# A hybrid attention layer: another buffer for v's turned tiles, weight splits kept, output weights issued earlier, and the next rows' squares moved to another stage

## The chip, the cores and the metric

One Trainium2 chip, one of its cores. The time is the device time of one execution in microseconds, the median of three runs. Five engines work side by side: TensorE (PE), VectorE (DVE), ScalarE (ACT), GpSimd (POOL) and SyncE (SP), which here issues every DMA. Each takes its own instructions in the order in which they were issued to it.

## The reference, cut to what matters

One decoder layer: 16 learned meta tokens stand ahead of 2048 tokens of width 1024; after a norm, one projection makes the queries, keys and values of two attention branches and four sets of gates. One branch is stick-breaking attention (8 heads), the other sliding-window attention over 128 tokens with sinks (16 query heads on 2 key and value heads).

```
def rms_norm(x, g):
    y = xf * lax.rsqrt(jnp.mean(xf * xf, axis=-1, keepdims=True) + RMS_EPS)
...
xn = rms_norm(h, norm_gain[l])
proj = xn @ w_in[l]
sb_q, sb_k, sb_v, sw_q, sw_k, sw_v, sb_z, sw_z, g_sb, g_sw = jnp.split(proj, offsets, axis=-1)
...
# stick-breaking, per head
log_beta = jax.nn.log_sigmoid(z)                       # z = q k^T * scale
log_1m = jnp.where(mask, log_beta - z, 0.0)
rev = lax.cumsum(log_1m, axis=3, reverse=True)
w = jnp.where(mask, jnp.exp(log_beta + suffix), 0.0)   # suffix: rev shifted by one
```

Each branch's output is gated, projected to width 1024 and gated again; the two are added, projected by `w_out`, added to x, and normed once more.

## The kernel before, in words

All products of float32 operands are made as three products of their split parts: each operand is split into a high part and the rest (`h` and `l`), and TensorE forms h·h, l·h and h·l (in `gemm`, L404 to L406). A split costs a copy on ACT or POOL and a difference on DVE or POOL.

The 2048 tokens are four groups of 512, worked on in two halves, first groups 2 and 3, then groups 0 and 1. Each half has three stages:

- The sliding-window stage (`window`, `attend`): projection tiles of 128 columns, each a `gemm`, are woven with the attention of the window, row by row. Here v's tiles of the stick-breaking branch are made too: TensorE turns them into PSUM (`ps_zm`, L512), ACT and DVE write the high part and the rest into the tile `vt` (allocated at L513, in a ring of one buffer), and a DMA stores `vt` to `vd` in HBM.
- The stick-breaking stage (`stick`), woven with the tiles of the gates (`gts`). For each head and group, a state, the keys, values and queries are loaded: the queries twice, as `q1` and, with halves swapped, as `q2`, each from a ring of two buffers. A state's score rows (L813) go through ACT's sigmoid (L817) and DVE's running product (L824), are turned by TensorE (L835), split (L113, L114) and multiplied with v.
- The finish: the branch projections, the product with `w_out`, and the last norm.

The order of TensorE's instructions is written out by hand. DVE's is by hand at the start only; ACT, POOL and SP are ordered by a scheduler from the order of the text, with the buffer rings as a constraint. All DMAs stand in one queue on SP.

**Weights.** `weights` (L164) serves one tile of 128 columns: the first time it loads it (512 KB, ring `raw` of two buffers), splits it, and stores high part and rest to HBM; `kept` remembers where. A later call loads the two parts. `kept.pop` forgets a tile with the second call, so that a third call loads, splits and stores again. This concerns the eight tiles of the window's queries, which are called once for each group, four times in all; the others are called twice.

**Scales of x.** The norm needs each row's sum of squares. `squares` (L346) loads 128 rows by 512 columns at a time into the ring `xs` (four buffers, which the window stage uses too), squares them on ACT with an accumulated sum, and `rsqrt` (L116) makes the scale: a logarithm (L119), an exponential (L120) and a step of refinement. For the second half's two groups, `group_scales` is called in the first half, after the tenth gate tile of the stick-breaking stage; with the ring as it is, the scheduler puts the squares into the end of the window stage before.

**Output weights.** In the finish, `w_out` is used in two column halves. `out_weights(k, ch)` loads one of eight 128-row tiles (ring `a` of six buffers), casts it on ACT (L234) and subtracts on DVE (L235). The first column half is prepared during the projection before. The second is issued after both row tiles (t = 0 and 1) of the first column half. For each row tile: TensorE's product (L280 to L282), DVE's addition of x into `res` (L284), ACT's square (L288).

Of the kernel before, what the change touches and what calls it, by code (L numbers as in the profile page):

```python
# [16 lines left out]
P = 128  # L17
# [27 lines left out]
def tile_kernel(ctx, tc, x, xt, meta, metat, gain, w_in, w_sb, w_sw, w_out, sinks, fgain,  # L45
# [67 lines left out]
        A.activation(h, acc, AF.Copy, scale=scale)  # L113
        V.scalar_tensor_tensor(l, acc, scale, f32(h), op0=ALU.mult, op1=ALU.subtract)  # L114

    def rsqrt(r, ssq, pool, mid=lambda: None):  # L116

        V.tensor_scalar(ssq, ssq, 1.0 / D, EPS, op0=ALU.mult, op1=ALU.add)
        A.activation(r, ssq, AF.Ln)  # L119
        A.activation(r, r, AF.Exp, scale=-0.5)  # L120
        mid()
        t = pool.tile([P, 4], F32, tag="nwt", name="nwt", bufs=2)[:r.shape[0], :r.shape[1]]
        V.tensor_tensor(t, r, r, op=ALU.mult)
        V.tensor_tensor(t, t, ssq, op=ALU.mult)
        V.tensor_scalar(t, t, -0.5, 1.5, op0=ALU.mult, op1=ALU.add)
        V.tensor_tensor(r, r, t, op=ALU.mult)
# [23 lines left out]
    def drain(*gens):  # L150
        for _ in chain(*gens):
            pass
# [11 lines left out]
    def weights(c0, w=w_in, raw=None):  # L164

        if c0 in ready:
            return ready.pop(c0)
        n = w.shape[2]
        wh, wl = (wp.tile([P, KT, P], F32R, tag=t, name=t, bufs=3)[:, :n, :] for t in ("wh", "wl"))
        key = w.name, c0  # L170
        if key in kept:
            for t, k in zip((wh, wl), kept.pop(key)):
                DMA(t, k)
            return wh, wl
        raw = load(c0, w) if raw is None else raw
        split(wh, wl, raw)
        kept[key] = [dram(f"{t}_{w.name}_{c0}", [P, n, P], F32R) for t in "hl"]
        for t, k in zip((wh, wl), kept[key]):
            if put_off is None:
                DMA(k, t)  # L180
            else:
                put_off.append((k, t))
        return wh, wl
# [19 lines left out]
    def finish(ringl, osw, first):  # L203
# [23 lines left out]
        for half, groups in enumerate(halves):  # L227
            part, merged, wo = {}, {}, {}

            def out_weights(k, ch):  # L230
                raw = small("a", AB)
                DMA(raw, w_out[0, k * P:(k + 1) * P, ch * GT:(ch + 1) * GT])
                h, l = wo[k, ch] = ringr(), ringr()
                A.copy(h, raw)  # L234
                V.tensor_tensor(l, raw, f32(h), op=ALU.subtract)  # L235
# [29 lines left out]
            for g in groups:  # L265
                for t0 in range(0, 4, 2):
                    res, ssq = {}, {}
                    end = (half, g, t0) == (1, groups[1], 2)
                    for ch in range(2):
                        cs = slice(ch * GT, (ch + 1) * GT)  # L270
                        for t in (t0, t0 + 1):
                            row = g * GT + t * P
                            if ch == 0:
                                res[t] = cp.tile([P, D], F32, tag="xr", name="res", bufs=3)
                                DMA(res[t], x[row:row + P, :])
                            acc = bank()
                            ts = slice(t * P, (t + 1) * P)
                            for k in range(KT):
                                (mh, ml), (wh, wl) = merged[k, g], wo[k, ch]
                                T.matmul(acc, lhsT=mh[:, ts], rhs=wh, start=k == 0, stop=False)  # L280
                                T.matmul(acc, lhsT=mh[:, ts], rhs=wl, start=False, stop=False)
                                T.matmul(acc, lhsT=ml[:, ts], rhs=wh, start=False, stop=k == KT - 1)  # L282
                            r = res[t][:, cs]
                            V.tensor_tensor(r, acc, r, op=ALU.add)  # L284
                            sq = cp.tile([P, GT], mybir.dt.bfloat16, tag="a", name="sq", bufs=AB)
                            if ch == 0:
                                ssq[t] = cp.tile([P, 2], F32, tag="ssq", name="ssq2", bufs=4)
                            A.activation(sq, r, AF.Square, accum_out=ssq[t][:, ch:ch + 1])  # L288
                            if end and t == 3:
                                V.tensor_tensor(r, r, fg[:, cs], op=ALU.mult)  # L290
                                if ch == 0:
                                    s0 = cp.tile([P, 1], F32, tag="rs", name="rs2", bufs=4)
                                    V.tensor_scalar(s0, ssq[t][:, 0:1], 1.0 / D, EPS, op0=ALU.mult, op1=ALU.add)
                        if (g, t0, ch) == (groups[0], 0, 0):
                            for k in range(KT):
                                out_weights(k, 1)
                    for t in (t0, t0 + 1):
                        row = g * GT + t * P
                        if end and t == 3:
                            s1 = ssq[t][:, 1:2]  # L300
                            rs, u = (cp.tile([P, 1], F32, tag="rs", name="rs2", bufs=4) for _ in range(2))
                            A.activation(rs, s1, AF.Ln, bias=s0, scale=1.0 / D)
                            A.activation(rs, rs, AF.Exp, scale=-0.5)
                            V.tensor_scalar(u, s1, 1.0 / D, s0, op0=ALU.mult, op1=ALU.add)
                            V.scalar_tensor_tensor(u, rs, rs, u, op0=ALU.mult, op1=ALU.mult)
                            V.tensor_scalar(u, u, -0.5, 1.5, op0=ALU.mult, op1=ALU.add)
                            a, b = (res[t][:, ch * GT:(ch + 1) * GT] for ch in range(2))
                            A.activation(a, a, AF.Copy, scale=rs)
                            V.tensor_scalar(b, b, rs, u, op0=ALU.mult, op1=ALU.mult)
                            DMA(out[row:row + P, GT:], b)  # L310
                            A.activation(a, a, AF.Copy, scale=u)
                            DMA(out[row:row + P, :GT], a)
                            continue
                        V.tensor_tensor(ssq[t][:, 0:1], ssq[t][:, 0:1], ssq[t][:, 1:2], op=ALU.add)
                        rs = cp.tile([P, 1], F32, tag="rs", name="rs2", bufs=4)
                        rsqrt(rs, ssq[t][:, 0:1], cp)
                        for ch in range(2):
                            cs = slice(ch * GT, (ch + 1) * GT)
                            V.scalar_tensor_tensor(res[t][:, cs], res[t][:, cs], rs, fg[:, cs], op0=ALU.mult, op1=ALU.mult)
                        DMA(out[row:row + P, :], res[t])  # L320
                if half == 0:
                    g2 = halves[1][g - groups[0]]
                    osw2.update({(k, g2): gated(ow, zw, k, g2, ringl, lambda: small("a", AB)) for k in range(8)})
# [32 lines left out]
    def spread(rs, rows, n):  # L356
# [2 lines left out]
        for i in range(n):  # L359
            T.transpose(acc[:, i * rows:(i + 1) * rows], rs[:rows, i:i + 1].to_broadcast([rows, P]), ident[:rows, :rows])  # L360
        return acc[:, :n * rows]

    def group_scales(g, tag="rs"):
        return scales(squares(x[g * GT:(g + 1) * GT, :], P, 4), P, 4, tag)

    def scale_rows(rs, rb=None):
        if rb is None:
# [127 lines left out]
    def sb_v(p):  # L495

        def use(g, acc, ms):
# [11 lines left out]
            def rows():  # L509
                tr = ps("zm")  # L510
                for i in range(4):
                    T.transpose(tr[:, i * P:(i + 1) * P], d[:, i * P:(i + 1) * P], ident)  # L512
                vt = tp.tile([P, 4, 2, P], F32R, tag="vt", name="vt", bufs=1)  # L513
                evac_split(vt[:, :, :, 0:64], vt[:, :, :, 64:128], tr.rearrange("p (b a d) -> p b a d", b=4, a=2))
                DMA(vd[p][g].rearrange("a p b d -> p b a d"), vt)

# [238 lines left out]
        return sw_k, sw_v, sw_q, attend, ending  # L755


    def stick(groups, bp):
        kt, vc = {}, {}
        rows_of = {}  # L760
        for g in groups:
# [34 lines left out]
        def row(h, g, n, j):  # L796

            if n == j == 0:
                load_kv(h, g)
                state[h, g] = {"q": load_q(h, g), "last": {}}  # L800
            st = state[h, g]
            last = st["last"]
            b0 = 4 * (g + n) + j
# [236 lines left out]
    for half, groups in enumerate(halves):  # L1040
# [38 lines left out]
            flush_all()  # L1079
        with tc.tile_pool(name=f"sb{half}", bufs=1, side="left") as bp:  # L1080
            vsplit[0] = False
            side = stick(groups, bp)
            drain(tiles_by_tile(gts[3:4], groups))
            rest = 25 if half == 0 else 23
            cost_sb = 8 * sum(4 * (4 - g) for g in groups) * 1.31 + 16 * 0.75
            ratio = cost_sb / ((rest - 4) * 10.4)
            left = weave(tiles_by_tile(gts[4:14], groups), side, ratio)
            if half == 0:
                rs0, rs1 = (group_scales(g) for g in halves[1])
            weave(tiles_by_tile(gts[14:rest], groups), side, ratio, left)  # L1090
            drain(side)
        if half == 0:
            ts = [mk() for mk in gts[rest:]]
            drain(by_group(ts, groups[:1]), by_group(ts[:1], groups[1:]))
# [69 lines left out]
```

## Time and the profile before

| | |
|---|---|
| median of three runs | 2207.05 us (2206.35 to 2208.54) |
| the profiled execution | 2209.05 us, its span 2207.3 us |
| mean granted clock of TensorE in it | 0.994 |
| PE busy | 2160.9 us, 98% of the span |
| DVE, ACT, POOL busy | 1365.7, 1013.8, 380.2 us |
| window stage of the first half ends | at about 400 us; its stick-breaking stage at about 773 us |

The span runs from the first to the last instruction on the core. In rows of a timeline the first number is the start, the second the time that the instruction, or the run of equal instructions counted at the end, took; brackets hold how long the engine was idle before it and what released it. In rows of groups the three durations are the shortest, the median and the longest in nanoseconds. Waits are listed as the engine, the tile and the line that waited, then the engine, the tile and the line that ended the wait, then total, count and longest.

### The profile page before, as it was taken

The page shows a single profiled execution, that of the slowest core. Times are in us where ns is not written, and L with a number is a line of the kernel's source. Part 1 is how long each engine was busy: PE and PEld are TensorE (multiplying, and loading weights), DVE is VectorE, ACT ScalarE, POOL GpSimd, SP SyncE. Part 2 cuts the span into 40 slices and gives each one's busy share as a digit, 9 for nine tenths or more (in the row PEclk, how much of TensorE's full clock was granted, in tenths as well). Part 3 has the DMA queues.
Part 4 walks back from the last instruction along what each step waited for, and adds up shares of the span by engine and source line. Part 5 has one row for each costly group of instructions (what it writes and reads, how often), then busy time and mean ns, then how long its engine had stood idle before and what let it go on. Part 6 is the DMA issues. An engine that isn't in the chain of part 4 may idle for free.

```text
span 2207.3 us, 30283 instructions
## 1 busy us (share of the span) xinstructions
PE 2160.9 (98%) x10614; PEld 1771.3 (80%) x10614; DVE 1365.7 (62%) x2130; ACT 1013.8 (46%) x2332; POOL 380.2 (17%) x493
## 2 busy tenths in 40 slices
PE   8899999999999999999999999999999999999998
PEld 6678887788888888788887888888888888787876
DVE  6678876356555443778755888778774437453543
ACT  6566767333433323677753555555553202221121
POOL 2123342322222201233310000000000232000000
PEclk9999999999999999999999999999999999999999
DMA  9655446856455365544446433333323976467422
GB/s 335 232 175 189 172 171 210 261 182 203 161 179 180 130 232 181 172 172 151 155 135 196 120 110 113 116 99 112 115 84 129 348 271 212 147 221 271 151 91 86
DMA packets 175800, 384.61 MB, mean 174 GB/s; under 512 B 23040, under 2 KB 41216, under 8 KB 175648
## 3 DMA queue, kind: packets, MB, share of 16 engines
q1 hardware_dynamic: 175648, 382.67, 52.0%
q8 instruction: 84, 1.38, 0.3%
q14 instruction: 68, 0.56, 0.1%
HBM read 233.16 MB, written 149.37 MB: 173 GB/s over the span
## 4 chain that ended last, share of the span: by engine, by line
PE 77%; issue 2%; DVE 1%; DMA 1%; ACT 1%; POOL 0%; POOLq 0%; ACTq 0%; DVEq 0%
PE ps_g L404 12%; PE ps_g L405 12%; PE ps_g L406 12%; PE ps_o L861 6%; PE ps_z L813 6%; PE ps_t L835 5%; PE ps_o L722 1%; PE ps_z L676 1%; PE ps_g L224 1%; PE ps_g L225 1%; PE ps_z L225 1%; PE ps_g L223 1%; PE ps_z L223 1%; PE ps_z L224 1%; PE ps_t L225 1%
## 5 line engine op out<-in xcount | busy, mean ns | idle before, releaser
L404 PE MATMUL ps_g<-xh,wh 128*128 128x512 f32 x1544 | 639.2, 414 | 9.7 <-ACT xh L911 7.5
L405 PE MATMUL ps_g<-xl,wh 128*128 128x512 f32 x1544 | 609.2, 395 | 0.4 <-DVE xl L912 0.4
L406 PE MATMUL ps_g<-xh,wl 128*128 128x512 f32 x1544 | 608.9, 394 | 0.0
L824 DVE TENSOR_TENSOR_SCAN row<-row 128x512 f32<-128x512 f32 (+2 forms) x320 | 372.5, 1166 | 176.4 <-POOL row L822 105.1
L406 PEld LDWEIGHTS ps_g<-xh,wl 128*128 128x128 f32 x1544 | 291.7, 189 | 65.5
L404 PEld LDWEIGHTS ps_g<-xh,wh 128*128 128x128 f32 x1544 | 293.4, 190 | 57.3 <-ACT xh L911 7.5
L405 PEld LDWEIGHTS ps_g<-xl,wh 128*128 128x128 f32 x1544 | 293.2, 190 | 43.9 <-DVE xl L912 0.9
L817 ACT ACTIVATE row<-ps_z 128x512 f32<-128x512 f32 (+1 forms) x320 | 172.0, 538 | 276.2 <-PE ps_z L813 228.7
L114 DVE SCALAR_TENSOR_TENSOR wtl<-ps_t,wth 128x512 fp32r<-128x512 f32 (+1 forms) x320 | 189.8, 593 | 42.9 <-ACT wth L113 41.4
L113 ACT ACTIVATE wth<-ps_t 128x512 fp32r<-128x512 f32 (+1 forms) x320 | 170.4, 532 | 97.4 <-PE ps_t L835 95.8
L813 PE MATMUL ps_z<-kt,q 128*128 128x512 f32 (+3 forms) x640 | 185.0, 369 | 0.3 <-ACT row L817 0.3
L835 PE MATMUL ps_t<-ident,row 128*128 128x128 f32 x1088 | 171.6, 273 | 1.2 <-DVE row L824 1.2
L835 PEld LDWEIGHTS ps_t<-ident,row 128*128 128x128 f32 x1088 | 135.9, 140 | 37.3 <-DVE row L824 1.7
L109 POOL TENSOR_SCALAR wh<-raw 128x1024 fp32r<-128x1024 f32 (+1 forms) x71 | 75.8, 1067 | 437.6 <-PE ps_g L405 303.7
L822 POOL TENSOR_SCALAR_AFFINE_SELECT row<-row 128x128 f32<-128x128 f32 x128 | 44.1, 346 | 619.0 <-ACT row L817 584.0
L813 PEld LDWEIGHTS ps_z<-kt,q 128*128 128x128 f32 x640 | 118.7, 188 | 26.4 <-ACT row L817 0.8
L861 PE MATMUL ps_o<-wth,vc 128*128 128x512 f32 (+1 forms) x320 | 125.7, 393 | 1.3 <-DVE tmp L866 1.1
L552 ACT ACTIVATE tmp<-ps_g 128x512 f32<-128x512 f32 x112 | 67.1, 599 | 121.0 <-PE ps_g L406 113.9
L684 ACT ACTIVATE sc<-sc,nm 128x129 f32<-128x129 f32 x256 | 100.0, 392 | 37.0 <-DVE nm L682 36.4
L861 PE MATMUL ps_o<-wtl,vc 128*128 128x512 f32 (+1 forms) x320 | 116.8, 365 | 0.0
L110 POOL TENSOR_TENSOR wl<-raw,wh 128x1024 fp32r<-128x1024 f32 (+1 forms) x43 | 96.4, 2242 | 3.1
L262 ACT CAST ringl<-gt 128x512 fp32r<-128x512 f32 x32 | 19.9, 621 | 132.0 <-DVE gt L260 128.0
(293 smaller groups left out, 3457.8 us busy)
## 6 DMA issues: line engine op xcount, KB each, us to landing
raw<-in_w_in SPq DMA_DIRECT2D x58, 512.0 KB, 4.5
h_in_w_in<-wh SPq DMA_DIRECT2D x58, 512.0 KB, 3.2
l_in_w_in<-wl SPq DMA_DIRECT2D x58, 512.0 KB, 3.4
wh<-h_in_w_in SPq DMA_DIRECT2D x58, 512.0 KB, 3.7
wl<-l_in_w_in SPq DMA_DIRECT2D x58, 512.0 KB, 4.8
q<-qd SPq DMA_DIRECT2D x128, 128.0 KB, 3.4
vc<-vd SPq DMA_DIRECT2D x48, 256.0 KB, 2.7
kd<-tmp SPq DMA_DIRECT2D x32, 256.0 KB, 4.1
```

The costliest lines, as they stand in the source:

```text
L110: (V if vsplit[0] else G).tensor_tensor(l, src, f32(h), op=ALU.subtract)
L113: A.activation(h, acc, AF.Copy, scale=scale)
L114: V.scalar_tensor_tensor(l, acc, scale, f32(h), op0=ALU.mult, op1=ALU.subtract)
L404: T.matmul(acc, lhsT=wh[:, k, :], rhs=xh[g][:, k, :], start=k == 0, stop=False)
L405: T.matmul(acc, lhsT=wh[:, k, :], rhs=xl[g][:, k, :], start=False, stop=False)
L406: T.matmul(acc, lhsT=wl[:, k, :], rhs=xh[g][:, k, :], start=False, stop=k == KT - 1)
L684: A.activation(sc[:, hh, :], sc[:, hh, :], AF.Exp, bias=nm[:, hh:hh + 1], accum_out=den[:, hh:hh + 1])
L813: T.matmul(z[:, :w], lhsT=lq, rhs=kt[h][:, k0:k0 + w], start=t == 0, stop=t == 1)
L817: A.activation(r[:, :w], z[:, :w], AF.Sigmoid, scale=-1.0)
L824: V.tensor_tensor_scan(r[:, :w], r[:, :w], r[:, :w], last[j] if n else 1.0, op0=ALU.mult, op1=ALU.min)
L835: T.transpose(tr[:, j * P:(j + 1) * P], rows_of[h, g, n - (j > i), j][:, k0:k0 + P], ident)
L861: T.matmul(o[:, :n], lhsT=v, rhs=r, start=first and r is wh, stop=last and r is wl)
```

## The change

Four edits:

1. `vt` comes, in the second half (groups 0 and 1), from the ring `raw` of the weights, which has two buffers; in the first half it keeps its own single buffer.
2. `kept[key]` in place of `kept.pop(key)`: a third and fourth call of a tile load the stored parts. With this no weight tile of the input projection is loaded raw in the second half's window stage.
3. The second column half's `out_weights` are issued right after the first row tile's square, ahead of the second row tile.
4. `group_scales` is gone. `stick` takes one 128 by 512 square of x with each of its 16 states (8 heads, 2 groups): load and square in a tile `xq` from the ring of `q2`, the sum into that group's `ssq`. After the stage, one `rsqrt` on eight columns makes both groups' scales, in a tile `rs8`, with its two scratch tiles from the ring of the split rows. The weaving of the gate tiles is one call instead of two. The order of TensorE's instructions is the same in both kernels.

```
-            for t, k in zip((wh, wl), kept.pop(key)):
+            for t, k in zip((wh, wl), kept[key]):
...
                             A.activation(sq, r, AF.Square, accum_out=ssq[t][:, ch:ch + 1])
+                            if (g, t, ch) == (groups[0], 0, 0):
+                                for k in range(KT):
+                                    out_weights(k, 1)
...
-                        if (g, t0, ch) == (groups[0], 0, 0):
-                            for k in range(KT):
-                                out_weights(k, 1)
...
-                vt = tp.tile([P, 4, 2, P], F32R, tag="vt", name="vt", bufs=1)
+                if g < 2:
+                    vt = wp.tile([P, 4, 2, P], F32R, tag="raw", name="vt", bufs=2)
+                else:
+                    vt = tp.tile([P, 4, 2, P], F32R, tag="vt", name="vt", bufs=1)
...
-    def stick(groups, bp):
+    def stick(groups, bp, sums_of={}):
...
                 state[h, g] = {"q": load_q(h, g), "last": {}}
+                n1 = len(state) - 1
+                for g1, ssq in list(sums_of.items())[n1 // 8:n1 // 8 + 1]:
+                    i, f = divmod(n1 % 8, 2)
+                    t = bp.tile([P, GT], F32, tag="q2", name="xq", bufs=2)
+                    DMA(t, x[g1 * GT + i * P:g1 * GT + (i + 1) * P, f * GT:(f + 1) * GT])
+                    A.activation(t, t, AF.Square, accum_out=ssq[:, f, i:i + 1])
...
-            side = stick(groups, bp)
+            next_sums = {g: sums() for g in halves[1]} if half == 0 else {}
+            side = stick(groups, bp, next_sums)
...
-            left = weave(tiles_by_tile(gts[4:14], groups), side, ratio)
+            weave(tiles_by_tile(gts[4:rest], groups), side, ratio)
+            drain(side)
             if half == 0:
-                rs0, rs1 = (group_scales(g) for g in halves[1])
-            weave(tiles_by_tile(gts[14:rest], groups), side, ratio, left)
-            drain(side)
+                t, u = (bp.tile([P, GT], F32, tag="wh", name="sum", bufs=3)[:, :8] for _ in range(2))
+                for n, ssq in enumerate(next_sums.values()):
+                    V.tensor_tensor(t[:, 4 * n:4 * n + 4], ssq[:, 0], ssq[:, 1], op=ALU.add)
+                rs = tp.tile([P, 8], F32, tag="rs8", name="rs", bufs=1)
+                rsqrt(rs, t, tp, t=u)
+                rs0, rs1 = rs[:, :4], rs[:, 4:]
```

## The prediction

> **What bounds the kernel now.** I read the page first (busy times), then the windows (stage by stage), then PE's waits, and then the instructions around each wait.
>
> ```profile
> span 2207.3 us, 30283 instructions
> ...
> PE 2160.9 (98%) x10614; PEld 1771.3 (80%) x10614; DVE 1365.7 (62%) x2130; ACT 1013.8 (46%) x2332; POOL 380.2 (17%) x493
> ```
>
> TensorE is busy for 2160.9 of 2207.3 us; no other engine comes near. Both kernels issue the same matmuls in the same order, written out by hand, so the change can only win what TensorE loses between them: 2207.3 - 2160.9 = 46.4 us of idle time, and what a lowered clock costs after idle time. The windows show where it lies. Columns: stretch, its length, then busy time and count for PE, weight loads, DVE, ACT and POOL, then the granted clock, DMA share and GB/s.
>
> ```profile
> 350.00:375.00 25.00, 21.20 (x104) 16.19 (x102) 14.34 (x28) 16.03 (x50) 4.88 (x8) 1.00 0.80 266
> 375.00:400.00 25.00, 23.57 (x90) 18.18 (x91) 7.86 (x23) 19.21 (x37) 6.50 (x7) 0.86 0.75 241
> 400.00:757.00 357.00, 357.00 (x1807) 294.11 (x1806) 192.02 (x239) 135.22 (x278) 100.52 (x110) 1.00 0.57 183
> 900.00:912.00 12.00, 9.38 (x38) 7.41 (x37) 9.70 (x18) 9.91 (x29) 1.59 (x1) 0.86 0.38 134
> 1888.00:1900.00 12.00, 9.83 (x35) 7.21 (x34) 6.60 (x12) 5.90 (x12) 0.00 (x0) 0.86 0.24 74
> 2110.00:2120.00 10.00, 8.01 (x35) 6.12 (x33) 1.51 (x3) 1.90 (x6) 0.00 (x0) 1.00 0.09 26
> 2120.00:2132.00 12.00, 11.39 (x45) 8.47 (x46) 8.06 (x17) 5.13 (x12) 0.00 (x0) 1.00 0.23 68
> ```
>
> Four places bear on the change. The end of the first half's sliding-window stage (350 to 400) is idle for 3.80 + 1.43 = 5.23 us and runs at clock 0.86 for 25 us, which I read as 0.14 x 25 = 3.5 us lost: 8.7 at stake. The same place of the second half (900 to 912): 2.62 idle and 0.14 x 12 = 1.68 of clock, 4.3 at stake. The start of the output projection, once per half: 1888 to 1900 has 2.17 + 1.68 = 3.85, and 2110 to 2132 has 1.99 + 0.61 = 2.6. Together 19.5 us. The stick-breaking stage between (400 to 757) has no idle time at all: whatever is put there wins nothing, and can only lose.
>
> **Squares out of the window stage.** Before, all 16 squares of the next half's x (L346) and two rsqrts (L119, L120) fall into the end of the window stage, since their buffers come free only there.
>
> ```profile
> L55 SPq DMA_DIRECT2D xs<-in_x x16: 327/333/1191, 342.3 to 385.3; - x16
> L346 ACT ACTIVATE xs<-xs x16: 616/630/634, 345.0 to 389.9; 128x512 f32<-128x512 f32 x16
> L346 ACT ACTIVATION_READ_ACCUMULATOR xs<-xs x16: 185/187/193, 345.6 to 390.4; 128x1 f32 x16
> ...
> DMA to landing us min/median/max: 2.8/3.6/7.1
> ```
>
> ```profile
> 367.71 0.63 ACT L346 ACTIVATE xs<-xs 128x512 f32<-128x512 f32 x1 [0.26 <-DMA xs<-in_x]
> 368.34 0.25 ACT L679 COPY sc<-ps_z 128x32 f32<-128x32 f32 x2
> 372.56 0.58 ACT L724 COPY tmp<-ps_o 64x512 f32<-64x512 f32 x1
> 378.85 1.28 ACT L119 ACT_TABLE_LOAD   x1
> 385.29 0.60 ACT L113 ACTIVATE ph<-ps_t 128x512 fp32r<-128x512 f32 x1
> 371.42 0.39 PE L405 MATMUL ps_g<-xl,wh 128*128 128x512 f32 x1
> 371.65 0.39 PE L406 MATMUL ps_g<-xh,wl 128*128 128x512 f32 x1
> 374.38 0.47 PE L722 MATMUL ps_o<-ph,vv 128*128 128x512 f32 x1 [2.34 <-DVE os L728]
> 385.94 0.50 PE L722 MATMUL ps_o<-ph,vv 128*128 128x512 f32 x1 [0.35 <-ACT ph L113]
> ```
>
> ACT runs strictly in turn here: the copy of the scores at 368.34 stands behind a square that waited for its transfer, and everything up to TensorE's 2.34 us wait follows from that copy (scores, exponentials, the copy L724 at 372.56, DVE's L728). Later `ph` stands behind squares and table loads of 1.28 us. In the changed order none of these is left between the attention's copies on ACT: 16 x (0.63 + 0.19) = 13.1 us and four table loads (5.1) leave a stretch of 45 us. Following the order of the changed kernel with these durations, `ph` is ready before TensorE asks for it; the first wait keeps perhaps 0.5, because DVE still has a weight split in that chain. I take 8.0 of 8.7; ends 5.5 (the copies are late for their own chain) and 8.7.
>
> One more loss goes with each wait. Back to back, matmuls of 0.39 us start 0.23 apart (371.42, 371.65); after a wait this overlap of 0.16 is gone, which busy time hides. In the four stretches that is about 12 waits of which I let 10 go: 1.6 us; ends 0 and 2.
>
> **v's turned tiles in two buffers.**
>
> ```profile
> 890.13 0.60 PE L512 MATMUL ps_zm<-ident,tmp 128*128 128x128 f32 x4
> 892.49 0.60 ACT L113 ACTIVATE vt<-ps_zm 128x512 fp32r<-128x512 f32 x1 [6.04 <-DMA vd<-vt]
> 905.73 0.69 DVE L600 SCALAR_TENSOR_TENSOR tmp<-ps_g,ct 128x512 f32<-128x512 f32 x1 [1.51 <-ACT tmp L599]
> 907.54 0.77 DVE L680 COPY_PREDICATED sc<-sel,ps_z 128x256 f32<-128x256 int32 x2
> 906.47 0.50 PE L404 MATMUL ps_g<-xh,wh 128*128 128x512 f32 x1 [2.02 <-DVE tmp L600]
> 908.03 2.07 PE L676 MATMUL ps_z<-kk,q 128*128 128x256 f32 x8 [0.60 <-DVE sc L680]
> ```
>
> ACT stood 6.04 us for the store of the tile before (one buffer), with the rotations' copies queued behind it; TensorE pays 2.02 and 0.60 us some 14 us later. With the second buffer the activation needs only TensorE's turned values, done at 890.13 + 0.60, 1.7 us before 892.49, so the chain moves up by 1.7, not by 6.04. The 2.02 falls to about 0.3, the 0.60 to about 0.4; part of the clock loss goes. I take 2.7 of 4.3 (1.9 idle, half of 1.68); ends 1 and 4.3. The first half keeps one buffer, so its waits stay.
>
> **Output weights sooner.** Eight casts and eight differences make the first output weights of the second column half; before, they follow the second row tile's square.
>
> ```profile
> PE ps_z L280 <- ACT ringr L234: 4.2, 2, 2.1
> ```
>
> ```profile
> L55 SPq DMA_DIRECT2D a<-in_w_out x8: 327/404/1731, 1881.7 to 1891.8; - x8
> ...
> DMA to landing us min/median/max: 3.2/4.0/4.1
> ```
>
> ```profile
> 1888.47 0.69 DVE L284 TENSOR_TENSOR res<-ps_g,res 128x512 f32<-128x512 f32 x1 [4.91 <-PE ps_g L282]
> 1889.25 0.63 ACT L288 ACTIVATE sq<-res 128x512 bf16<-128x512 f32 x1 [4.88 <-DVE res L284]
> 1889.88 3.40 ACT L234 CAST ringr<-a 128x512 fp32r<-128x512 f32 x6
> ```
>
> ACT idles 4.88 us for the second square while the loaded weights lie there: issued from 1881.7, landed about 4.0 later, from 1885.7. Now the first casts (3.40 / 6 = 0.57 each) run in that idle time and are done by 1888, when TensorE wants them; both waits of 2.1 us go, with their low clock. The second square is late by a few casts, and nobody on TensorE asks for it soon. At stake 3.85 + 2.6 = 6.45; I take 6.0, since the last two of the eight still wait for ring slots; ends 4 and 6.5.
>
> **What is added in the stick-breaking stage.** One square of x per head and group (16 states) takes a slot in the two-slot ring of the queries' swapped copy `q2`, so the next state's `q2` waits for the square, and the square for the last use of the one before.
>
> ```profile
> L55 SPq DMA_DIRECT2D q<-qd x8: 467/570/587, 448.4 to 462.6; - x8
> ...
> DMA to landing us min/median/max: 2.6/2.9/5.3
> ```
>
> ```profile
> 448.36 0.47 SPq L55 DMA_DIRECT2D q<-qd  x1
> 451.08 0.39 PE L813 MATMUL ps_z<-kt,q 128*128 128x512 f32 x1
> 464.38 0.63 PE L813 MATMUL ps_z<-kt,q 128*128 128x512 f32 x2
> ```
>
> The shorter states last 464.38 - 451.08 = 13.3 us. Their slot came free at 448.36, and the next queries are wanted at 464.38: 16.0 us. In that go about 1.2 us on SP's queue (two issues of 0.57 ahead), x landing in 3.6, the square 0.82, two issues of 0.57, and 2.9 to land: 9.7. With the longest landings seen, 7.1 and 5.3, it is 15.6: it still fits. The longer states have twice the time. Behind the waiting transfers SP's queue holds weights (wanted tiles later) and stores; behind the waiting square ACT holds the rows' sigmoids and the splits of the turned rows. At the median landing the square waits about a microsecond or not at all, at 7.1 about 4, and TensorE has two score buffers of some 3 us each before it stops. ACT is 38% busy here (135.22 of 357), 42% with the squares. I put 0.5 us on it; ends 0 and 6. The one rsqrt at the stage's end falls where ACT waits for the last rows.
>
> **Weights stay kept.** Eight tiles are not split a second time: eight loads, sixteen stores, eight casts and eight differences less, sixteen loads more.
>
> ```profile
> raw<-in_w_in SPq DMA_DIRECT2D x58, 512.0 KB, 4.5
> ```
>
> None of TensorE's waits names a weight tile, so I cost it at 0; ends -1 and +1.
>
> **The sum.** 8.0 + 1.6 + 2.7 + 6.0 - 0.5 = 17.8 us. The profiled run took 2209.05 (1.75 around its span), so 2191.3; it was 2.0 above the median of 2207.05, so the median should be 2189.3: I give 2189. With all low ends: 5.5 + 0 + 1 + 4 - 6 - 1 = 3.5 less; with all high ends 8.7 + 2 + 4.3 + 6.5 + 1 = 22.5 less.
>
> **Rivals.** *The clock does not come back.* Then 3.5, 0.84 (half of 1.68) and 1.68, 6.0 us in all, are not won: 2195. For it: the loss may have other causes than these waits. Against it: the clock reads 0.86 right where 2 us waits lie, and 1.00 throughout 400 to 757, where nothing waits. The window 900 to 912 is the test: its two waits are 2.02 and 0.60, apart, and the clock fell. In "TensorE: Matmul & The Clock Gate" (section on the HAM clock gate) the Trainium skill says that throttling comes after an idle window of about 3.4 us; by that rule waits of 2 us like these would not throttle, and the clock loss would stay whatever the change does, as this rival has it. The rows with 2 us waits speak against it. Chance 0.08.
>
> *The window stage stays late without squares.* Then its waits come from its own chain (scores, exponentials, table switches, DVE's splits), and only half of 8.0 and of one us of overlap is won: 2189.3 + 4.5 = 2194. For it: the 2.34 us wait names DVE, not ACT, and the weight split lies in that chain. Against it: the copy at 368.34 stood right behind a square. Chance 0.15.
>
> *The ring of the queries takes the gain back.* If x lands so late that the next queries miss their first use (over about 7.5 us with queries landing in 5.3, or over about 10 with 2.9), the eight shorter states each wait. At 2 us each, with 0.16 of overlap and 1.7 us of clock as at 1888, that is 8 x 3.9 = 31 us against 17.8 + 0.5 won: 2207 + 13 = 2220, slower. For it: the chain has 0.4 us to spare at the worst rows, and ACT's turn can add to it. Against it: 7.1 was seen at DMA share 0.80, and this stage has 0.57. Chance 0.08.
>
> *The moves change nothing.* The output weights still wait for their transfers, and the freed ACT time falls to other waits: about 2205, chance 0.04.
>
> **How the numbers follow.** Forecast 0.65, rivals 0.15, 0.08, 0.08, 0.04. The forecast's own range is 2185 to 2193 and the first two rivals end at 2195; with some ACT waiting in the added work (up to 6) the range is 2184 to 2200, which leaves out the slower rival and the last. A difference of 0.2% (4.4 us) is about what can be told from none here. Faster: 0.65 + 0.15 + 0.08 = 0.88, less 0.01 for the case that two rivals come together: 0.87; same 0.04 + 0.01 = 0.05; slower 0.08.
>
> **What would show it.** Right: no L346 between 340 and 400, clock 1.00 there and idle below 1 us; vt without a wait for `vd`; no PE wait at L280 for L234; 400 to 757 still without idle time; `raw` 50 times instead of 58. Wrong: waits of PE at L813 for `q`, or at L813 or L835 for ACT, between 400 and 757; an ACT wait on `xq` of over 4 us in many states; clock 0.86 remaining where the waits have gone.

## The result, and the profile after

The changed kernel takes 2189.26 us (2188.12 to 2192.93, four runs) where the kernel before takes 2206.7 in the same comparison: a ratio of 0.992, 95% interval 0.9905 to 0.9934. Measured again beside other kernels it took 2189.08 against 2207.29: 0.9915, 0.9901 to 0.9928. By the medians it is 17 to 18 us faster; 2189 was forecast.

The page of the changed kernel, its first part:

```profile
span 2187.8 us, 30234 instructions
...
PE 2153.3 (98%) x10614; PEld 1768.4 (81%) x10614; DVE 1357.2 (62%) x2117; ACT 1007.7 (46%) x2327; POOL 370.6 (17%) x485
```

The same 10614 matmuls. Idle time fell from 46.4 to 34.5 us, and busy time by 7.6, although the work is the same: a matmul in a lowered clock, or one that has just waited, counts as busy for longer (in the kernel before 0.63 us each at 1892, in the lowered clock, and 0.49 us after the wait at 2120, where 0.39 is usual). Busy time alone would have hidden almost 40% of the gain.

The windows at the places shown before. The output projections have moved to about 1876 and 2100.

```profile
350.00:375.00 25.00, 24.62 (x124) 19.75 (x123) 16.82 (x34) 15.03 (x44) 6.45 (x10) 1.00 0.70 234
375.00:400.00 25.00, 25.00 (x114) 20.62 (x113) 5.16 (x10) 4.77 (x9) 8.77 (x7) 1.00 0.69 230
400.00:757.00 357.00, 357.00 (x1817) 294.08 (x1816) 191.47 (x240) 143.68 (x311) 101.40 (x110) 1.00 0.58 191
890.00:912.00 22.00, 21.01 (x111) 17.14 (x109) 17.69 (x38) 17.22 (x56) 4.93 (x6) 1.00 0.35 120
1876.00:1888.00 12.00, 12.00 (x52) 9.29 (x51) 8.62 (x18) 5.90 (x13) 0.00 (x0) 1.00 0.23 80
2090.00:2112.00 22.00, 22.00 (x96) 17.68 (x95) 11.93 (x24) 7.97 (x18) 0.00 (x0) 1.00 0.26 79
```

Every one of these places is full or nearly so, at clock 1.00, and the stick-breaking stage, with 16 squares more in it, is still without idle time. In 890 to 912 one microsecond stays idle.

Since TensorE's instructions stand in the same order in both kernels, each matmul can be set against itself. How much earlier (minus) or later it starts than in the kernel before, at some times of the kernel before, worked out from the two traces:

```
                  at 340    420     890     920    1880    1902    2105    2135 us
changed           +0.92   -8.63   -8.77  -11.74  -11.59  -15.49  -15.88  -19.53
changed again     +2.17   -7.54   -7.60  -10.59  -10.48  -14.64  -14.90  -18.56
```

The differences between neighbours are the terms: the window stage's end -9.55 (again: -9.71), v's tiles -2.97 (-2.99), the output weights -3.90 (-4.16) and -3.65 (-3.66). From 420 to 890, where the squares now are, the shift hardly moves. Before 340 the kernels hardly differ, and the shift there goes with the clock (below). A shift sets one profile against one other, so a term also holds what the profile of the kernel before happened to lose at that place; how much that is, the other profiles of unchanged code show (also below).

### The profile page after: what moved, and what is told of

Same layout as the page of the kernel before. It is cut to its first block, busy times and chain, and to the rows that moved or that the text cites. A ratio compares the mean times of both kernels' runs of the same rounds, so it can differ in the third digit from the quotient of the medians.

```text
span 2187.8 us, 30234 instructions
## 1 busy us (share of the span) xinstructions
PE 2153.3 (98%) x10614; PEld 1768.4 (81%) x10614; DVE 1357.2 (62%) x2117; ACT 1007.7 (46%) x2327; POOL 370.6 (17%) x485
## 4 chain that ended last, share of the span: by engine, by line
PE 88%; DVE 2%; issue 2%; ACT 2%; DMA 1%; POOL 0%; POOLq 0%; SPq 0%; ACTq 0%; DVEq 0%
PE ps_g L402 15%; PE ps_g L403 14%; PE ps_g L404 14%; PE ps_o L868 6%; PE ps_z L820 6%; PE ps_t L842 5%; PE ps_o L723 2%; PE ps_z L677 2%; PE ps_g L225 1%; PE ps_g L226 1%; PE ps_z L226 1%; PE ps_g L224 1%; PE ps_z L224 1%; PE ps_z L225 1%; PE ps_t L226 1%
## 5 line engine op out<-in xcount | busy, mean ns | idle before, releaser
L109 POOL TENSOR_SCALAR wh<-raw 128x1024 fp32r<-128x1024 f32 (+1 forms) x63 | 66.7, 1059 | 357.6 <-PE ps_g L403 217.6
L603 POOL TENSOR_TENSOR tmp<-tmp 128x512 f32<-128x512 f32 (+1 forms) x37 | 47.7, 1290 | 195.3 <-DMA qd<-tmp 72.2
```

## The experiments

Ratios are against the kernel before as it was timed beside each: 2205.8 us for the first four kernels, 2208.58 for v's tiles alone, for the rsqrts written later and for the squares done twice or three times, 2207.29 for the other four.

**Each edit alone.** Five kernels, each the kernel before with one or two of the edits.

The squares alone (`stick` takes them one by one, `group_scales` gone; the other edits undone):

> Only the fourth edit (squares of x one by one in the stick-breaking stage), the other three undone. My theory, that the parts add and the end of the first half's window stage is freed: TensorE's idle time between 340 and 400 us falls from 5.2 to about 0.4 us, the start of every later matmul moves by about -9.5 us and stays there, so 2206.7 - 9.5 = about 2197. The rival, that the window stage keeps waits of its own and the gain of the whole change came from elsewhere: less than 5 us, above 2202. The rival of the queries' ring: waits at L820 between 400 and 757, less than 5 us too.

Measured: 2197.35 us (2195.34 to 2201.08), ratio 0.9964 (0.9949 to 0.9979). The shift goes from -2.67 at 340 to -12.25 at 420: -9.58, as in the full change, and stays within half a microsecond up to 1902; between 400 and 800 TensorE has no wait. TensorE's waits between 340 and 400, in the kernel before and then in this one (total, count, longest):

```profile
PE ps_o L722 <- DVE os L728: 2.9, 2, 2.3
PE ps_o L722 <- POOL cl L709: 1.4, 2, 0.8
PE ps_o L722 <- DVE pl L114: 0.6, 3, 0.3
PE ps_o L722 <- ACT ph L113: 0.3, 1, 0.3
```

```profile
PE ps_o L720 <- DVE pl L114: 0.2, 1, 0.2
```

All but 0.2 us has gone; the window stage had no wait of its own behind the squares.

The output weights alone:

```
+                            if (g, t, ch) == (groups[0], 0, 0):
+                                for k in range(KT):
+                                    out_weights(k, 1)
```

> Only the third edit (output weights issued after the first row tile's square). My theory: both waits of 2.1 us at L280 and what follows them go, -3.9 us in the first half and -3.6 in the second, together -7.5: about 2199. The rival, that the weights still wait for their loads or that the second square now comes late: less than 4 us.

Measured: 2202.02 us, ratio 0.9975 (0.9964 to 0.9987); shifts of -3.93 from 1880 to 1902 and -3.65 from 2105 to 2135. The time alone doesn't decide: the medians differ by 3.8 us, inside the rival's less than 4, and the ratio allows 2.9 to 7.9. The trace does: both waits at L280 are gone. In the changed kernel ACT goes like this at the first of the two places:

```profile
1875.27 3.23 ACT L235 CAST ringr<-a 128x512 fp32r<-128x512 f32 x5 [2.50 <-DMA a<-in_w_out]
1878.56 0.63 ACT L289 ACTIVATE sq<-res 128x512 bf16<-128x512 f32 x1
1879.19 1.76 ACT L235 CAST ringr<-a 128x512 fp32r<-128x512 f32 x3
```

Five casts stand ahead of the second square, in time that was idle, and the last three after it are in time too. The margin is small: the first cast starts 1.4 us before TensorE would ask for it. In the seven profiles with this edit the gain at the first place runs from 2.3 to 4.2 us, with short waits for these casts where it is small; at the second it is 3.65 in all seven.

The kept parts alone, and together with v's tiles:

```
-            for t, k in zip((wh, wl), kept.pop(key)):
+            for t, k in zip((wh, wl), kept[key]):
```

> Only the second edit (kept parts are not forgotten). My theory: no TensorE wait names a weight tile, so 0 within 1 us: 2206.7. The rival, that the eight splits spared are what frees the second half's window stage (900 to 912): about -3, 2203.7.

> The first and the second edit (v's turned tiles in the ring of the weights, kept parts not forgotten). My theory: the start of matmuls after 912 us moves by -3.0 us: 2203.7. If the kept parts alone give the same as this, the buffer of v's tiles does nothing; if they give nothing, the buffer does it all, or both are needed.

Measured: 2206.56 us, ratio 1.0002 (0.9989 to 1.0015), and 2205.93, ratio 1.0 (0.9989 to 1.001). Kept alone, the shift at 890 to 920 is +0.07: nothing. With v's tiles it is -3.02. The time doesn't show these 3 us, which are no more than its interval; the trace does. This pair of edits is therefore shown as a shift, not as a time.

v's tiles alone, with the tiles of weights still split a second time:

> The first edit alone: v's turned tiles of the second half in the ring of the raw weights, which is still used by the eight query tiles that are split again. My theory, that the second buffer is what counts and that the raw loads come after v's tiles in that stage: matmuls after 912 us move by -3.0 us as with both edits. The rival, that the ring must be idle: a tile of v waits for the split of a raw tile or holds up the next raw load, ACT waits before the tile again, and the shift after 912 is between -1.5 and +3 us.

Measured: 2217.98 us, ratio 1.0045 (1.0023 to 1.0066): slower. My theory held for a few microseconds and then fell. From 890 to 912 the shift goes by the same -3.0, but at 1000 it stands at +11.4. TensorE's waits on the way:

```profile
914.70 0.50 PE L404 MATMUL ps_g<-xh,wh 128*128 128x512 f32 x1 [0.71 <-POOL wh L109]
919.48 0.79 PE L406 MATMUL ps_g<-xh,wl 128*128 128x512 f32 x1 [4.04 <-DVE wl L110]
935.59 0.79 PE L406 MATMUL ps_g<-xh,wl 128*128 128x512 f32 x1 [4.90 <-DVE wl L110]
```

These are weights that are split again. The splits on POOL, in the kernel before and then here:

```profile
891.28 1.05 POOL L109 TENSOR_SCALAR wh<-raw 128x1024 fp32r<-128x1024 f32 x1 [10.77 <-PE ps_g L405]
898.55 1.23 POOL L109 TENSOR_SCALAR wh<-raw 128x1024 fp32r<-128x1024 f32 x1
```

```profile
913.61 1.04 POOL L109 TENSOR_SCALAR wh<-raw 128x1024 fp32r<-128x1024 f32 x1
928.59 1.05 POOL L109 TENSOR_SCALAR wh<-raw 128x1024 fp32r<-128x1024 f32 x1
```

and SP's queue here:

```profile
885.90 6.54 SPq L55 DMA_DIRECT2D vd<-vt  x2
897.16 0.73 SPq L55 DMA_DIRECT2D vm<-tmp  x1
897.99 0.38 SPq L55 DMA_DIRECT2D raw<-in_w_in  x1
915.55 0.60 SPq L55 DMA_DIRECT2D vd<-vt  x1
```

A raw load takes its turn in the ring with v's tiles. The first is issued only at 897.99, after two stores of `vt` (in the kernel before the load was issued at 843.07); it landed 9.5 us later and, in POOL's turn, is split at 913.61, 22 us later than in the kernel before; the next is issued at 919.87, after the store at 915.55. The product then waits for the split. So the second edit, worth nothing by itself, is what makes the first possible.

**Squares or table loads?** The window stage's end held two things on ACT: the squares with their transfers, and the table loads of the two rsqrts. First, on the kernel before: the squares as they were, the rsqrts written after the stage.

```
-                rs0, rs1 = (group_scales(g) for g in halves[1])
+                sq0, sq1 = (squares(x[g * GT:(g + 1) * GT, :], P, 4) for g in halves[1])
...
             drain(side)
+            if half == 0:
+                rs0, rs1 = (scales(s, P, 4) for s in (sq0, sq1))
```

> The kernel before with one move: the two rsqrts of the next half's scales, with their four or more table loads of 1.28 us, stand after the stick-breaking stage, while the 16 squares stay where they were. If the table loads make the loss between 340 and 400 us, most of the 9.5 us go (5 to 8). If the squares and their transfers ahead of the attention's copies make it, as I argued for the first wait, less than 4 us go, and the wait of 2.3 us on os at about 374 stays.

Measured: 2208.79 us, ratio 0.9997 (0.9987 to 1.0007). It decides nothing: the trace has all four table loads of L119 and L120 between 377.98 and 391.77, where they were. The scheduler placed the rsqrts when their sums were ready, not where they are written. So, second, the scratch tiles of one joint rsqrt come from the stage's own ring (`wh`, as in the changed kernel), which is free only at its end.

> The kernel before, with the 16 squares where they were and one rsqrt on eight columns after the stick-breaking stage, its scratch tiles taken from that stage's ring, so that it cannot start earlier. In the order of ACT, four loads at L119 and L120 and the loads that switch back leave the stretch 340 to 400; one load at L552 stays. If the squares and their transfers make the loss, as I argued, the shift of TensorE between 340 and 420 is -1 to -4 us and the 2.3 us wait on os stays. If the table loads make it, -6 to -9.5. Half of each would be -4 to -6.

Measured: 2205.55 us, ratio 0.9996 (0.9986 to 1.0005). Now the trace has one table load in the stretch, where the kernel before has seven (two each at L119 and L120, three at L552), and the waits and the windows are:

```profile
PE ps_o L722 <- DVE os L728: 2.6, 1, 2.6
PE ps_o L722 <- POOL cl L709: 1.2, 2, 0.8
PE ps_o L722 <- DVE pl L114: 0.2, 1, 0.2
```

```profile
350.00:375.00 25.00, 21.79 (x109) 17.08 (x107) 14.66 (x30) 16.87 (x52) 5.50 (x9) 1.00 0.85 283
375.00:400.00 25.00, 24.14 (x101) 19.30 (x102) 6.59 (x12) 10.92 (x26) 8.33 (x8) 0.93 0.79 257
```

The wait for `os` stays, the shift from 340 to 420 is -3.44. So of 9.55 us the rsqrts with their table loads make about 3.4 and the squares with their transfers about 6.1: the larger part, as argued. The profile of the kernel before lost more than others at this place: five others with the same squares and rsqrts here (the output weights alone, the kept parts with and without v's tiles, v's tiles alone, the rsqrts written later) gain 0.68 to 0.93 us on it between 340 and 420. Against them the whole is 8.6 to 8.9 us and the rsqrts' part 2.5 to 2.8; the 6.1 stay. The squares moved with the rsqrts left here, and why the waits for `cl` (POOL's splits) go with the squares, were not tried.

**How much room the queries' ring has.** In the changed kernel, the load and the square of `xq` are done twice or three times in turn, in the same tile:

```
+                    for _ in range(3):                      # or 2
                         DMA(t, x[g1 * GT + i * P:g1 * GT + (i + 1) * P, f * GT:(f + 1) * GT])
                         A.activation(t, t, AF.Square, accum_out=ssq[:, f, i:i + 1])
```

> The changed kernel with each load and square of xq done twice in turn in the same tile (the sums are those of the last). It doubles what stands in the ring of the queries. By my chain: 1.2 on the queue, 2 x (4.3 + 0.82) with the landing now measured, 0.5 for the second issue, 1.1 and 2.9 for the queries: 16.0 us against 16.0 us in the short states, so at the edge: 0 to 8 x 1 us, and TensorE between 400 and 757 idle for 0 to 8 us. By the rival, that ACT's turn decides: ACT is held some 7 us in each state, more than two score buffers of 3 us, and TensorE waits 1 to 3 us in each of 16 states: +16 to +48 us.

> The changed kernel with each load and square of xq done three times in turn. By my chain 21.6 us against 16.0 in the eight short states: late by 5 to 6 us each, with the clock some 7: +40 to +60 us, and the long states untouched. If ACT's turn decides instead, all 16 states wait, 6 to 9 us each: +100 us or more. If the scheduler moves the squares back far enough, or the chain has more room than I reckoned, below +15 us.

Measured: 2193.01 us with two, ratio 0.9929 (0.9912 to 0.9947), where the changed kernel has 2189.26 and 0.992; 2210.23 with three, ratio 1.0008 (0.9995 to 1.002). Against the changed kernel, the shift between 420 and 757 is +3.9 and +24.75. TensorE's waits between 400 and 800, with two and then with three:

```profile
PE ps_o L869 <- DVE tmp L874: 2.0, 1, 2.0
PE ps_t L843 <- DVE wtl L114: 1.4, 1, 1.4
```

```profile
PE ps_z L821 <- DMA q<-qd: 9.3, 6, 2.2
PE ps_zm L854 <- ACT row L827: 4.4, 1, 4.4
PE ps_o L869 <- DVE tmp L874: 3.0, 3, 1.8
PE ps_t L843 <- DVE wtl L114: 2.2, 1, 2.2
```

With two, the queries are never late. The two waits name DVE, but DVE's work there, followed back, hangs on rows and splits of ACT that stood behind a square: ACT had been idle for x for 3.82 and 1.60 us up to 462.29, some 8 us ahead of the first wait's end, and for 3.37 us up to 667.73, 5 us ahead of the second's. With three, the queries asked for during six of the eight short states come late, by up to 2.2 us, and half of the idle time ends with values of ACT, or of DVE behind ACT. So both rivals exist: ACT's turn shows with one square more in each state, the ring of the queries with two. The 21.6 us of my chain was too long, since the x now landed in 3.5 us (median of the seven landings on record), not 4.3: 1.2 + 3 x (3.5 + 0.82) + 1.0 + 1.1 + 2.9 = 19.2, against 16.0; measured, 2.2 late.

The same with three, but `xq` in a ring of its own:

> The changed kernel with each load and square of xq done three times, as before, but with xq in a ring of its own of two buffers, so that the queries keep their two. If the ring's chain made the loss of the run with three, the waits of TensorE at L821 for q go and the loss against the changed kernel falls from 21 us to below 8. If ACT's turn made it, the waits on row, tmp and wtl stay and the loss stays above 15 us.

Measured: 2209.84 us, ratio 1.0008 (0.9998 to 1.0018), as slow. No wait for q is left, but TensorE now waits 10.8 us at L869, for DVE's `tmp`, which waits for ACT's copy, and 2.5 us at L821 for ACT's rows. The two groups for `xq` say why, three times in the queries' ring first, then in its own:

```profile
L808 ACT ACTIVATE xq<-xq x48: 629/632/637, 395.3 to 749.2; 128x512 f32<-128x512 f32 x48
```

```profile
L808 ACT ACTIVATE xq<-xq x48: 614/632/634, 396.7 to 536.8; 128x512 f32<-128x512 f32 x48
```

With its own ring nothing ties a square to its state, and the scheduler pulls all 48 into the first 140 us. By the letter of what was expected this says that ACT's turn makes the loss; but the squares were spaced differently, so the two parts are not separated by it. What it does show: the ring of the queries also spaces the squares.

**The first two edits in company.** The changed kernel without them, beside the changed kernel:

> The changed kernel without its first two edits: the squares and the output weights alone. By the shifts of the traces -9.55 and -7.6: 17.1 us less than before; the two edits left out are worth 3.0 us, so it should lie 3 us above the changed kernel in the same call. If the shift at 912 us does not reach the time, the two are equal within 1 us.

> The changed kernel once more, beside the kernel without its first two edits. By the shifts of the traces 20.1 us less than before, 3.0 us less than its neighbour; the first measurement was 17.4 less.

Measured: 2191.11 us (2187.64 to 2193.47), ratio 0.9925 (0.9912 to 0.9937), against 2189.08 (2187.3 to 2190.51), ratio 0.9915 (0.9901 to 0.9928). The 2.0 us are of the size expected, but the ranges overlap, so the time doesn't show them. By the shifts it loses what v's tiles bring (-0.22 in place of -2.97 between 890 and 920), and 1.6 of the first output projection, where TensorE waits 0.67 and 0.23 us for the first weights. Why they came later is open: the landings on record, a median of 5.2 us there against 3.0 and 3.6 in the two profiles of the changed kernel, are one to three of eight, and with 5.4 the output weights alone lost nothing. By their ratios the squares alone and the output weights alone win 7.9 and 5.5 us, together 13.4, and the two in one kernel 16.6; the intervals are wide enough to hold both.

## Why the prediction was right

Its mechanisms held, one by one; most of the sizes were somewhat low, and errors cancelled.

- **The window stage.** 8.0 us without the overlap; measured 9.55 with it, or 8.6 to 8.9 against the five other profiles, so the 8.0 was about right. The 0.5 left for DVE's split was too much: 0.2 of waits are left in that wait's place. That the larger part is the squares' and their transfers' is shown. The prediction set no price on the table loads apart, and it counted four (5.1 us) where six go, since two at L552 switch back (388.11 and 394.73 in the kernel before).
- **v's tiles.** 2.7 without the overlap; measured 2.97. The point was that the chain moves up by 1.7 us, not by the 6.04 for which ACT stood, and this is what came: `vt` no longer waits for `vd`, only for TensorE's turned values, and starts at 882.00 where it started at 892.49; less the shift of -8.77 that the place already had, 1.72 us earlier.

```profile
882.00 0.60 ACT L113 ACTIVATE vt<-ps_zm 128x512 fp32r<-128x512 f32 x1 [4.30 <-PE ps_zm L510]
```

The waits left were put at 0.3 and 0.4, and are:

```profile
896.07 0.50 PE L402 MATMUL ps_g<-xh,wh 128*128 128x512 f32 x1 [0.39 <-DVE tmp L601]
897.63 1.22 PE L677 MATMUL ps_z<-kk,q 128*128 128x256 f32 x8 [0.60 <-DVE sc L681]
```

The second did not shrink at all (0.60 before). The clock, of which I gave back half, came back whole.

- **The output weights.** 6.0 of 6.45; measured 3.90 + 3.65 = 7.55. Here the amount at stake was mis-sized, since I counted the second half's waits as 1.99 + 0.61 = 2.6 and set 0.16 for the overlap behind each. In the rows of before at 2120 the loss is 3.65: after the wait of 2.09 the next matmuls start 0.72 and 0.34 apart, where 0.23 is usual, and two more start late when the rest of the weights arrive.

```profile
2120.11 0.49 PE L280 MATMUL ps_z<-ringr,ringl 128*128 128x512 f32 x1 [2.09 <-ACT ringr L234]
2120.83 0.49 PE L281 MATMUL ps_z<-ringr,ringl 128*128 128x512 f32 x1 [0.23 <-DVE ringr L235]
2121.17 0.40 PE L282 MATMUL ps_z<-ringr,ringl 128*128 128x512 f32 x1
```

The first half's 3.85 met the measured 3.90 partly by luck: it put 1.68 of it down to the clock, but in two profiles whose clock stayed at 1.00 there (the kept parts alone, v's tiles alone) the shift over this place is only -0.45 and -0.74. The late starts, for which the sum had 0.16 per wait, make up the rest. The residual of the last two weights, 0.45, did not show.
- **The added squares.** 0.5; measured 0.0 as shift between 420 and 757. But their transfers were slower than the row I took:

```profile
L55 SPq DMA_DIRECT2D xq<-in_x x16: 338/536/733, 393.1 to 714.5; - x16
L807 ACT ACTIVATE xq<-xq x16: 631/632/636, 397.5 to 717.1; 128x512 f32<-128x512 f32 x16
...
  DMA xq<-in_x: 30.1, 15
...
DMA to landing us min/median/max: 4.2/4.3/5.7
```

4.3 us to land (three of the 16 landings are on record), not 3.6, and ACT idle for 2.0 us per square (30.1 / 15), where I said a microsecond or none. ACT's reserve covered it.

- **Weights kept.** 0; measured +0.07 alone. `raw` is loaded 50 times, as forecast. The step was right and incomplete: it did not say that v's tiles depend on this edit, which the run without it shows at 11.9 us (shift at 1880, +11.86).
- **The sum.** 17.8 forecast, 20.1 measured as shifts (9.55 + 2.97 + 7.55), or 19.1 to 19.4 with the window stage set against the five other profiles. The medians differ by 17.4 and 18.2. Most of the remainder is not the change's: the profiled run of before was 2.35 us above its median of 2206.7 (0.7 to 0.9 of this in the window stage, by the five other profiles), and the changed one lost 0.92 before 340 us. So the 2189.0 was met more closely than its terms deserve: that part was luck.
- **The clock rival** is refused by the window stage and by v's tiles: the clock there is 1.00 once the waits have gone. But the prediction's own rows held a wait of 2.09 us at clock 1.00 (2110 to 2132), which it did not weigh: a wait of this length does not always lower the clock (below). The Trainium skill says in "TensorE: Matmul & The Clock Gate" (section on the HAM clock gate) that throttling follows an idle window of some 3.4 us; by that rule alone v's tiles would have gained no clock. The runs here disagree, since waits of 2.1 us were followed by a lowered clock.

## What to carry to other kernels

When one engine is full and its order is fixed, count what it loses at each place (idle time, the clock, and the late starts after each wait), and compare matmul by matmul: shifts resolve 3 us where medians of runs do not. Take more than one profile for it, since profiles with the same code at a place differed there by one to two microseconds. Work that falls into a burst because its buffers come free there costs more through its place than through its length: moved one by one to where its engine has idle time, 13 us of squares cost nothing, and 13 us more cost 4. A buffer borrowed from another ring is free only while that ring is idle; check who else takes a turn in it.

## What the runs showed of the hardware

**A wait of 2.1 us lowers the clock sometimes.** The wait at L280 is the same in the kernel before and in six of the experiments that leave it (2.09 to 2.11 us each time), but the clock is not. First and second half, the kernel before and then the run with the rsqrt held back:

```profile
1860.00:1910.00 50.00, 47.83 (x198) 37.72 (x197) 31.00 (x56) 15.31 (x32) 1.92 (x2) 0.97 0.59 193
2100.00:2140.00 40.00, 37.40 (x158) 29.05 (x157) 21.02 (x42) 12.51 (x28) 0.00 (x0) 1.00 0.32 105
```

```profile
1860.00:1910.00 50.00, 47.90 (x198) 37.85 (x197) 28.26 (x53) 14.90 (x32) 0.00 (x0) 0.97 0.55 188
2100.00:2140.00 40.00, 37.69 (x154) 29.75 (x153) 19.48 (x40) 10.91 (x26) 0.00 (x0) 0.96 0.31 101
```

Over these seven profiles it fell in five of the first waits and in two of the second. The two waits of 2.0 and 0.6 us near 907, one soon after the other, lowered it in all seven profiles that have them. Some four to eight matmuls then start 0.43 us apart instead of 0.23. Where it fell in the second, the kernel lost only 0.7 us more at that place than the kernel before, and 0.9 to 1.5 more than the four others whose clock stayed: the slower matmuls use up time in which the next weights were still awaited, and the late starts that the kernel before has at 2125 are absent.

**The early clock makes most of the scatter ahead of the change.** In all fourteen profiles the clock between 70 and 80 us, where the code is the same, reads 0.66 or 0.83, and between 90 and 100 from 0.66 to 1.00. The shift at 340 us, before any edit acts, follows the clock of the stretch from 60 to 140: -2.67 at 0.96, -0.97 to +0.45 at 0.94, +0.39 to +0.92 at 0.91, +0.87 to +2.17 at 0.89. That is as much as the first two edits are worth.
